# A two-layer encoder trunk on one core: q and k kept by head pair, an epsilon scaled by the frame's mean square, and the softmax sums' tiles moved to another pool

## The chip, the cores and the metric

The kernel runs on one core of one Trainium2 chip. The metric is device time in microseconds (us) of one execution. Engines: TensorE (PE, with its weight loads shown as PEld), VectorE (DVE), ScalarE (ACT), GpSimd (POOL), and SyncE (SP), which issues the DMAs.

## The reference, cut to what matters

Two residual layers on x (512 frames, 1024 channels, float32). Layer 0 mixes tokens with trailing means, layer 1 with chunked attention; each is followed by a gated MLP of 2816 hidden channels with a causal convolution over three frames.

```python
def rmsnorm(x, g):
    y = xf * lax.rsqrt(jnp.mean(xf * xf, axis=-1, keepdims=True) + EPS)      # EPS = 1e-6
    return y * g

def chunk_attention(h, w_qkv, q_norm, k_norm, rel_table, w_o):
    q, k, v = jnp.split(h @ w_qkv, 3, axis=-1)                 # 16 heads of 64
    q = head_rmsnorm(q, q_norm)                                # mean of squares over a head's 64, + EPS
    k = head_rmsnorm(k, k_norm)
    # each chunk of 64 frames attends to its own and the 8 chunks before it
    s = einsum(q, k) * HEAD_DIM ** -0.5 + bias[rel]
    return einsum(softmax(s), v) @ w_o

def conv_ffn(h, w_gate, w_val, conv_w, conv_b, w_out):
    a = causal_dwconv3(h @ w_gate) + conv_b
    return (silu(a) * (h @ w_val)) @ w_out

for i in range(2):
    x = x + mixer_i(rmsnorm(x, mix_norm[i]))
    x = x + conv_ffn(rmsnorm(x, ffn_norm[i]), ...)
```

In layer 1 the attention's input h is x times the frame's factor r = rsqrt(mean square of the frame + EPS) times the gain. Because r is one number for a frame, q and k can be projected from x times the gain alone, and the head norms then take r into account.

## The kernel before, in words

**Arithmetic.** Each matmul in full precision is made of three (`mm3`, L123 to L125): the operands are split into a high and a low part (`split`, L102 and L103: ScalarE copies the high part, VectorE subtracts; `split_scaled`, L107 and L108, does it with a factor), and high times high, high times low and low times high are added up in one bank of PSUM. Moving tiles are 128 x 512 (512 frames, 2048 bytes for each partition).

**FFNs (`ffn`).** The first few of the 22 blocks f of 128 hidden channels are plain products of the normed input (`plain`, 512-wide matmuls only). From f = 5 on Strassen's scheme takes seven products of half size a block (`strassen`, `product`, L594 and L596: four 512-wide matmuls with the high weights and both parts of the moving half, four 256-wide ones with the low weights). Between the products the schedule places matmuls of the output projection of an earlier group of blocks (`output`, names `out`, `ow`, `wo_r`), three or six at a time. All orders of TensorE are written by hand there. The moving tiles are `two` and `h` (normed input), `one` and `u` (hidden values).

**Attention (`attention`).** `opening` projects v by Strassen and the first quarter of q and k (c = 0; a quarter holds four heads of q and the same four of k, 512 columns). `project(c)` does the other quarters while the heads run: `products` issues the matmuls, `evict(t)` copies the bank of frame tile t (128 frames by 512 columns) to `Z[c, t]`, on VectorE for odd t and ScalarE for even t, and puts `squares(t)` and then `norms()` into the list `late`, from which the loop over heads and frame tiles takes one entry after a step. `squares` takes the squares (ScalarE) and sums them by head (VectorE, L1302). `norms` makes the factor: sum times `r2` (r squared over 64, L1317), plus EPS (L1318), rsqrt (L135 to L139), times r (L1320), and GpSimd then multiplies `Z[c, t]` by it for t = 0 to 3 (L1322; L1212 in `opening`). `channel_major(p, i)` transposes pair p (two heads) of q (i = 0) or k (i = 1) on TensorE, four transposes `zt` (L1365) that read the pair's 128 columns from `Z[p // 2, t]`, and splits the result (L107 and L108, or L1369 and L1372).

For each head and frame tile: `scores` (L1395, L1396; bias and maximum on VectorE, L1399; exponential on ScalarE, L1405, which also sums into a column of `sums[p]`), two steps later `turn` (transposes `tp`, L1436, split into `pt`), two more later `mix` (products `oo` with v, L1448). `sums_out`, `sums_in` and `scale` bring the inverse sums to the channels' layout through DRAM. Work that fills TensorE between: quarter 1's rest, quarters 2 and 3, and the output projection `wo`. TensorE's order is written by hand; of the other engines the planner orders the heads' part. Four PSUM banks (tag "S") serve scores, `zt`, `tp`, `rt` and `oo` in turn.

**Memory.** Pools open one behind the other, and a tile's place follows from the sizes of those before it: `consts` (ending at 18,432 bytes for each partition), `wp` (seven tiles of 4096 bytes: raw weights `wr`, and the halves `wh` and `wl`, two each), `act` (`X`, `one`, `two`), then `tmp`: `fill1` (128), five small norm columns and four-column tiles (128 and 128), six `g` tiles of 2048, four `mx` (32 each), two `sums` (32 each). Behind tmp come, at different times, the pools of the start (`pw` and others), of the first FFN (`h`, `gv` and `ow` halves), of the attention (`kl`, `zqk`, then `pre`, then `heads` with `pt`, `B`, `sb`, `o2`, `rs`, `rb`) and of the second FFN. The first FFN's `u` tiles and later `Z` lie in pools counted from the top of memory. `LINE` is 512 and `CONST` 128.

Of the kernel before, what the change touches and what calls it, by code (L numbers as in the profile page):

```python
# [30 lines left out]
HD = 64  # L31
NPAIR = H // 2
TT = S // P
# [3 lines left out]
EPS = 1e-6  # L37
# [4 lines left out]
LINE, CONST = 512, 128  # L42
# [30 lines left out]
def trunk(ctx: ExitStack, tc: tile.TileContext, xt, xT, cols, band, edge, poolw, gv, wout, wqk, wv, wo, rel, out):  # L73
    nc = tc.nc
# [3 lines left out]
    tmp = ctx.enter_context(tc.tile_pool(name="tmp", bufs=1))  # L78
# [62 lines left out]
    def small(name, n, tag="nw"):  # L141
        return tmp.tile([P, n], F32, name=name, tag=f"{tag}{n}", bufs=4)
# [211 lines left out]
    ident = consts.tile([P, P], F32, name="ident")  # L354
# [561 lines left out]
    def attention(rest, hook, hidden_slots):  # L916
        XS = set2
        O2, V, Z, QK, SM = {}, {}, {}, {}, {}
# [9 lines left out]
        def by_frame(v):  # L928
            return v.rearrange("p (t h) -> p t h", t=TT)

        zp = None

        def opening(pre):
# [3 lines left out]
            Y, SQ, sums, form = {}, {}, {}, {}  # L937
# [87 lines left out]
            def lo(n):  # L1025
                part_lo(f"v{n}")
# [33 lines left out]
            zp = closing.enter_context(tc.tile_pool(name="bz", bufs=1, side="right", reuse_waits="tile"))  # L1060
# [5 lines left out]
            ov = [psum("S", f"qk0_{t}", 4) for t in range(TT)]  # L1066
# [64 lines left out]
            a, rcol, t_ = (small(f"n1_{c}", TT) for c in "ayt")  # L1131
# [5 lines left out]
            nc.vector.scalar_tensor_tensor(t_, rcol, -0.5, rcol, op0=OP.mult, op1=OP.mult)  # L1137
            nc.vector.tensor_mul(t_, t_, a)
            nc.vector.scalar_tensor_tensor(rcol, t_, 1.5, rcol, op0=OP.add, op1=OP.mult)
            nc.vector.scalar_tensor_tensor(r2, rcol, 1.0 / HD, rcol, op0=OP.mult, op1=OP.mult)  # L1140
            lo(0)
            query(3)


            ss, a, y, t_ = norms_of(0)
            for t in range(TT):
                Z[0, t] = zp.tile([P, 8, HD], F32, name=f"z0_{t}", tag="z", bufs=8)
            flat = [Z[0, t].rearrange("p h d -> p (h d)") for t in range(TT)]
            zsq = {}

            def square(t):
                zsq[t] = g_tile(f"zs0_{t}")
                nc.scalar.activation(zsq[t], flat[t], AF.Square)

            def reduce(t):
                nc.vector.tensor_reduce(by_frame(ss)[:, t, :], zsq.pop(t).rearrange("p (h d) -> p h d", d=HD), axis=mybir.AxisListType.X, op=OP.add)
# [16 lines left out]
                return [vx(f"{name}{i}") for i in range(2)]  # L1173

            hi(1)
            nc.vector.tensor_copy(flat[1], ov[1])
            nc.scalar.activation(flat[0], ov[0], AF.Copy)
            nc.scalar.activation(flat[2], ov[2], AF.Copy)
            nc.vector.tensor_copy(flat[3], ov[3])
            square(0)  # L1180
            lo(1)
            half(0, A, "a11", True)
# [12 lines left out]
            reduce(2)  # L1195
            reduce(3)
            lo(3)
            nc.vector.tensor_mul(by_frame(a), by_frame(ss), r2[:, :, None].to_broadcast([P, TT, 8]))
            nc.vector.tensor_scalar(a, a, EPS, None, op0=OP.add)
            B = [psum("P", f"vb{i}") for i in range(2)]  # L1200
            half(2, B, "a12", True)
            hi(4)
# [7 lines left out]
            nc.vector.tensor_mul(by_frame(y), by_frame(y), rcol[:, :, None].to_broadcast([P, TT, 8]))  # L1210
            for t in range(TT):
                nc.gpsimd.tensor_mul(Z[0, t], Z[0, t], by_frame(y)[:, t, :, None].to_broadcast([P, 8, HD]))  # L1212
            half(3, B, "a12", True)
            hi(5)
            lo(5)
# [51 lines left out]
            c = pair_of("c12")  # L1267
# [25 lines left out]
        def project(c, banks="PQ", ready=None):  # L1293

            ov = [psum(banks[t // 2], f"qk{c}_{t}", BANKS[banks]) for t in range(TT)]
            ss, a, y, t_ = norms_of(c)
            s3, a3, y3 = (by_frame(v) for v in (ss, a, y))

            def squares(t):
                sq = g_tile(f"zs{c}_{t}")  # L1300
                nc.scalar.activation(sq, Z[c, t].rearrange("p h d -> p (h d)"), AF.Square)
                nc.vector.tensor_reduce(s3[:, t, :], sq.rearrange("p (h d) -> p h d", d=HD), axis=mybir.AxisListType.X, op=OP.add)  # L1302


            def evict(t):
                Z[c, t] = z = zp.tile([P, 8, HD], F32, name=f"z{c}_{t}", tag="z", bufs=8)
                flat = z.rearrange("p h d -> p (h d)")
                if t % 2:
                    nc.vector.tensor_copy(flat, ov[t])
                else:  # L1310
                    nc.scalar.activation(flat, ov[t], AF.Copy)
                late.append(lambda: squares(t))

            yield from products(ov, wqk[c], f"wqk{c}", nc.gpsimd, evict, ready)

            def norms():
                nc.vector.tensor_mul(a3, s3, r2[:, :, None].to_broadcast([P, TT, 8]))  # L1317
                nc.vector.tensor_scalar(a, a, EPS, None, op0=OP.add)  # L1318
                rsqrt(a, y, t_)
                nc.vector.tensor_mul(y3, y3, rcol[:, :, None].to_broadcast([P, TT, 8]))  # L1320
                for t in range(TT):
                    nc.gpsimd.tensor_mul(Z[c, t], Z[c, t], y3[:, t, :, None].to_broadcast([P, 8, HD]))  # L1322

            late.append(norms)

# [33 lines left out]
        def channel_major(p, i):  # L1359


            zt = psum("S", f"zt{p}_{i}", 4)
            for t in range(TT):
                j = 4 * i + 2 * (p % 2)
                nc.tensor.transpose(zt[:, t * P:(t + 1) * P], Z[p // 2, t][:, j:j + 2, :].rearrange("p h d -> p (h d)"), ident)  # L1365
# [12 lines left out]
            for o, x in moves:  # L1378
                nc.sync.dma_start(o.bitcast(F32), x if x.dtype == F32 else x.bitcast(F32))
            QK[p, i] = (zh, z2)  # L1380

        def scores(h, t):

            p, e = divmod(h, 2)
            q, k, kl = QK[p, 0][e], QK[p, 1][e], KL[p % 2][e]
            if t == 0:

                base = rdram[h, :]
                for r, n in ((0, S - HD), (HD, S)):
# [9 lines left out]
            nc.vector.tensor_tensor_reduce(out=s_[:, :n], in0=sc[:, :n], in1=BT[h % 2][:, :n][:, ::-1], scale=1.0,  # L1399
                                           scalar=3e38, op0=OP.add, op1=OP.min, accum_out=mx[:, 0:1])  # L1400
            if p < NPAIR - 1:
                if e == 0 and t == 0:
                    sums[p] = tmp.tile([P, 2 * TT], F32, name=f"sums{p}", tag="sums", bufs=2)
                c = e * TT + t
                nc.scalar.activation(s_[:, :n], s_[:, :n], AF.Exp, scale=-1.0, bias=mx[:, 0:1], accum_out=sums[p][:, c:c + 1])  # L1405
                if c == 2 * TT - 1:
                    nc.vector.reciprocal(sums[p], sums[p])
            else:
                nc.scalar.activation(s_[:, :n], s_[:, :n], AF.Exp, scale=-1.0, bias=mx[:, 0:1], accum_out=mx[:, 1:2])
                nc.vector.reciprocal(mx[:, 2:3], mx[:, 1:2])  # L1410
                nc.scalar.activation(s_[:, :n], s_[:, :n], AF.Copy, scale=mx[:, 2:3])
# [59 lines left out]
        with tc.manual_schedule(engines={mybir.EngineType.PE}):  # L1471
# [17 lines left out]
            for i in range(nb + LAG + LAGM):  # L1489
                steps = []  # L1490
                p = (i - 9) // 8
# [6 lines left out]
                j = i - LAG  # L1498
# [112 lines left out]
```

## Time and profile before

| | |
|---|---|
| time of the runs, us | 972.7, 973.65, 973.53 (median 973.53) |
| time of the profiled execution, us | 972.28 |
| its span, us | 970.5 |
| TensorE busy, share of the span | 99% |
| VectorE busy | 87% |
| ScalarE busy | 59% |
| GpSimd busy | 8% |
| granted TensorE clock | 1.000 |

The span is the time from the first to the last instruction of the profiled execution; 1.8 us of its time lie around it. The parts in order of time: the pool mixer to about 30 us, the first FFN to about 350 with its last outputs to about 372, the attention's opening to about 457, the heads to about 608, the second FFN to the end. In a row of the order of time the first number is the start, the second the time until the end of the row's last instruction; matmuls overlap, so the pace of TensorE is the distance from one start to the next and not the duration.

### The profile page before, as it was taken

The numbers are of one execution on the slowest core, as the hardware profiler recorded it, in microseconds if no ns is written. First come the engines' busy times: TensorE is split into PE (matmuls) and PEld (weight loads), VectorE is DVE, ScalarE is ACT, GpSimd is POOL, SyncE is SP. The second block draws the span as 40 slices with busy tenths as digits, with TensorE's granted clock in tenths as the row PEclk, the third lists the DMA queues.
The fourth block names the chain that finished last, engine by engine and source line by source line (L and its number), as shares of the span: only waits on it lengthen the run. The fifth ranks groups of instructions, "written<-read, shape, count | busy, mean of one in ns | idle before, by whom it ended". The sixth has DMA issues, their size and how long they took to land. (4 is left out here: it accounts for less than half of the span.)

```text
span 970.5 us, 13715 instructions
## 1 busy us (share of the span) xinstructions
PE 960.2 (99%) x4965; PEld 809.0 (83%) x4965; DVE 849.1 (87%) x1479; ACT 575.0 (59%) x980; POOL 80.5 (8%) x76
## 2 busy tenths in 40 slices
PE   8999999999999999999999999999999999999998
PEld 7788988888888888888888787888988888888886
DVE  8999999999899859894776988899999999899853
ACT  7665554655555457465777777656556555465521
POOL 2300000000000000033534310000000000000000
PEclk9999999999999999999999999999999999999999
DMA  9232332332323317024443442232233233233322
GB/s 342 70 99 71 114 108 80 120 119 81 114 79 120 102 47 292 20 66 134 143 122 108 129 118 67 90 121 84 75 114 119 72 121 127 84 103 91 105 82 103
DMA packets 40227, 105.73 MB, mean 109 GB/s; under 512 B 4744, under 2 KB 8272, under 8 KB 40160
## 3 DMA queue, kind: packets, MB, share of 16 engines
q1 hardware_dynamic: 40096, 104.82, 33.3%
q8 instruction: 39, 0.64, 0.3%
q14 instruction: 28, 0.23, 0.1%
q0 software_dynamic: 32, 0.04, 0.0%
q10 hardware_dynamic: 32, 0.00, 0.0%
HBM read 98.48 MB, written 2.17 MB: 104 GB/s over the span
## 5 line engine op out<-in xcount | busy, mean ns | idle before, releaser
L124 PE MATMUL out<-one,ow_h 128*128 128x512 f32 x224 | 88.6, 395 | 0.0
L123 PE MATMUL out<-one,ow_h 128*128 128x512 f32 x224 | 88.5, 395 | 0.0
L125 PE MATMUL out<-one,ow_l 128*128 128x512 f32 x224 | 88.4, 395 | 0.0
L830 DVE TENSOR_TENSOR X<-out,X 128x512 f32<-128x512 f32 (+1 forms) x65 | 44.1, 680 | 47.8 <-PE out L125 47.7
L594 PE MATMUL st_m<-two,g_h 128*128 128x512 f32 x240 | 75.5, 396 | 0.0
L594 PE MATMUL st_m<-h,g_h 128*128 128x512 f32 x240 | 75.1, 394 | 0.0
L393 ACT ACTIVATE ow_h<-wo_r 128x768 fp32r<-128x768 f32 (+1 forms) x56 | 44.5, 795 | 44.7 <-PE out L124 41.9
L408 DVE SCALAR_TENSOR_TENSOR c<-a,col,c 128x511 f32<-128x511 f32 (+1 forms) x76 | 56.4, 744 | 0.0
L594 PEld LDWEIGHTS st_m<-h,g_h 128*128 128x128 f32 x240 | 45.1, 188 | 10.6
L596 PEld LDWEIGHTS st_m<-two,g_l 128*128 128x128 f32 x240 | 45.1, 188 | 10.5
L594 PEld LDWEIGHTS st_m<-two,g_h 128*128 128x128 f32 x240 | 44.0, 188 | 10.5 <-ACT w L603 0.9
L394 DVE TENSOR_TENSOR ow_l<-wo_r,ow_h 128x768 fp32r<-128x768 f32 (+1 forms) x56 | 50.1, 895 | 2.2 <-ACT ow_h L393 2.2
L603 ACT ACTIVATE w<-st_m 128x512 f32<-128x512 f32 x30 | 18.0, 599 | 56.2 <-PE st_m L596 56.2
L596 PE MATMUL st_m<-two,g_l 128*128 128x256 f32 x240 | 47.7, 280 | 0.0
L596 PE MATMUL st_m<-h,g_l 128*128 128x256 f32 x240 | 47.6, 279 | 0.0
L125 PEld LDWEIGHTS out<-one,ow_l 128*128 128x128 f32 x224 | 42.1, 188 | 6.1
L123 PEld LDWEIGHTS out<-one,ow_h 128*128 128x128 f32 x224 | 42.1, 188 | 6.0
L124 PEld LDWEIGHTS out<-one,ow_h 128*128 128x128 f32 x224 | 42.1, 188 | 5.9
L1399 DVE CUSTOM_DVE_ANT_0 sb<-sc,B 128x128 f32<-128x128 f32 (+1 forms) x64 | 31.1, 485 | 15.7 <-PE sc L1396 11.0
L405 ACT ACTIVATE c<-a,col 128x512 f32<-128x512 f32 x38 | 30.7, 812 | 23.1 <-DVE a L752 21.6
L1405 ACT ACTIVATE sb<-sb,mx 128x128 f32<-128x128 f32 (+3 forms) x56 | 31.3, 559 | 17.8 <-DVE mx L1399 16.8
L393 ACT ACTIVATE g_h<-gv_r 128x1024 fp32r<-128x1024 f32 x32 | 33.7, 1054 | 12.3 <-DMA gv_r<-gv 9.8
(464 smaller groups left out, 3004.2 us busy)
## 6 DMA issues: line engine op xcount, KB each, us to landing
gv_r<-gv SPq DMA_DIRECT2D x86, 512.0 KB, 3.6
wo_r<-wout SPq DMA_DIRECT2D x32, 384.0 KB, 3.1
wo_r<-wout SPq DMA_DIRECT2D x32, 320.0 KB, 2.9
wqk_r<-wqk SPq DMA_DIRECT2D x12, 512.0 KB, 3.7
b<-wv SPq DMA_DIRECT2D x8, 512.0 KB, 7.0
wo_r<-wo SPq DMA_DIRECT2D x8, 512.0 KB, 3.4
xt<-xt SPq DMA_DIRECT2D x4, 512.0 KB, 5.9
X<-xT SPq DMA_DIRECT2D x8, 256.0 KB, 7.5
```

Of the source, the lines that this page charges most:

```text
L123: yield nc.tensor.matmul(o, sh, mh, start=first, stop=False, **how)
L124: yield nc.tensor.matmul(o, sh, ml, start=False, stop=False, **how)
L125: yield nc.tensor.matmul(o, sl, mh, start=False, stop=last, **how)
L393: nc.scalar.activation(hi[:, :n], raw[:, :n], AF.Copy)
L394: return hi, lo, lambda: nc.vector.tensor_sub(lo[:, :n], raw[:, :n], hi[:, :n].bitcast(F32))
L405: nc.scalar.activation(c, a, AF.Identity, scale=cw[2], bias=cw[3])
L408: nc.vector.scalar_tensor_tensor(c[:, j:], a[:, :S - j], cw[2 - j], c[:, j:], op0=OP.mult, op1=OP.add)
L594: nc.tensor.matmul(o, hi[:, c], B[i, name], start=first and i == 0, stop=False, **how)
L596: nc.tensor.matmul(o[:, 0], lo[:, c], B[i, name][:, 0], start=False, stop=i == 3, **how)
L830: nc.vector.tensor_add(X[d][:, fs], o[:, fs], X[d][:, fs])
L1399: nc.vector.tensor_tensor_reduce(out=s_[:, :n], in0=sc[:, :n], in1=BT[h % 2][:, :n][:, ::-1], scale=1.0, scalar=3e38, op0=OP.add, op1=OP.m ...
L1405: nc.scalar.activation(s_[:, :n], s_[:, :n], AF.Exp, scale=-1.0, bias=mx[:, 0:1], accum_out=sums[p][:, c:c + 1])
```

## The change

It has three parts. `Z[c]` becomes one tile for a quarter, laid out by group of 128 columns (pair of q, pair of q, pair of k, pair of k), then frame tile, then column; evictions and squares write and read four pieces of 128 columns, a transpose reads one piece, and GpSimd multiplies group by group, for all frames at once, in the order 0, 2, 1, 3. The head norm's factor is made from the sum over 64 plus `eps`, a tile of four columns that holds EPS times the frame's mean square (plus EPS), in one VectorE instruction; the multiplications by `r2` and by r are gone. The `sums` tiles, eight columns each, are taken from the pool `heads`, with 512 bytes each, and no longer from `tmp`.

```diff
+        def variance(a, ss):
+            nc.vector.scalar_tensor_tensor(by_frame(a), by_frame(ss), 1.0 / HD, eps[:, :, None].to_broadcast([P, TT, 8]), op0=OP.mult, op1=OP.add)
+        def normalise(c, y):
+            for g in (0, 2, 1, 3):
+                z = Z[c][:, g].rearrange("p t (e d) -> p t e d", e=2)
+                nc.gpsimd.tensor_mul(z, z, by_frame(y)[:, :, 2 * g:2 * g + 2, None].to_broadcast([P, TT, 2, HD]))
...
-            nc.vector.scalar_tensor_tensor(r2, rcol, 1.0 / HD, rcol, op0=OP.mult, op1=OP.mult)
+            nc.vector.tensor_scalar(eps, a, EPS, None, op0=OP.mult)
...
-                Z[0, t] = zp.tile([P, 8, HD], F32, name=f"z0_{t}", tag="z", bufs=8)
+            Z[0] = zp.tile([P, TT, TT, P], F32, name="z0", tag="z", bufs=2)
+            flat = [Z[0][:, :, t, :] for t in range(TT)]
...
             def evict(t):
-                Z[c, t] = z = zp.tile([P, 8, HD], F32, name=f"z{c}_{t}", tag="z", bufs=8)
+                if t == 0:
+                    Z[c] = zp.tile([P, TT, TT, P], F32, name=f"z{c}", tag="z", bufs=2)
+                z = Z[c][:, :, t, :]
...
             def norms():
-                nc.vector.tensor_mul(a3, s3, r2[:, :, None].to_broadcast([P, TT, 8]))
-                nc.vector.tensor_scalar(a, a, EPS, None, op0=OP.add)
+                variance(a, ss)
                 rsqrt(a, y, t_)
-                nc.vector.tensor_mul(y3, y3, rcol[:, :, None].to_broadcast([P, TT, 8]))
-                for t in range(TT):
-                    nc.gpsimd.tensor_mul(Z[c, t], Z[c, t], y3[:, t, :, None].to_broadcast([P, 8, HD]))
+                normalise(c, y)
...
-                nc.tensor.transpose(zt[:, t * P:(t + 1) * P], Z[p // 2, t][:, j:j + 2, :].rearrange("p h d -> p (h d)"), ident)
+                nc.tensor.transpose(zt[:, t * P:(t + 1) * P], Z[p // 2][:, 2 * i + p % 2, t, :], ident)
...
-                    sums[p] = tmp.tile([P, 2 * TT], F32, name=f"sums{p}", tag="sums", bufs=2)
+                    sums[p] = heads.tile([P, LINE // 4], F32, name=f"sums{p}", tag="sums", bufs=2)[:, :2 * TT]
...
-        r2, late, sums, RB = small("r2", TT), [], {}, {}
+        eps, late, sums, RB = small("eps", TT), [], {}, {}
```

`opening` changes in the same way for c = 0.

More of the change, by code (lines that the diff above doesn't have):

```diff
@@ L929, in by_frame, with heads_of @@
             return v.rearrange("p (t h) -> p t h", t=TT)
+        def heads_of(x):
+            return x.rearrange("p (g d) -> p g d", g=TT)
+        def variance(a, ss):
[4 more added lines that the diff above has]
+                nc.gpsimd.tensor_mul(z, z, by_frame(y)[:, :, 2 * g:2 * g + 2, None].to_broadcast([P, TT, 2, HD]))
         zp = None
@@ L1145, in opening @@
             ss, a, y, t_ = norms_of(0)
-            for t in range(TT):
-                Z[0, t] = zp.tile([P, 8, HD], F32, name=f"z0_{t}", tag="z", bufs=8)
-            flat = [Z[0, t].rearrange("p h d -> p (h d)") for t in range(TT)]
+            Z[0] = zp.tile([P, TT, TT, P], F32, name="z0", tag="z", bufs=2)
+            flat = [Z[0][:, :, t, :] for t in range(TT)]
             zsq = {}
@@ L1152, in square @@
                 zsq[t] = g_tile(f"zs0_{t}")
-                nc.scalar.activation(zsq[t], flat[t], AF.Square)
+                nc.scalar.activation(heads_of(zsq[t]), flat[t], AF.Square)
             def reduce(t):
@@ L1175, in opening @@
             hi(1)
[L1176 to L1179, printed above, removed]
+            nc.vector.tensor_copy(flat[1], heads_of(ov[1]))
+            nc.scalar.activation(flat[0], heads_of(ov[0]), AF.Copy)
+            nc.scalar.activation(flat[2], heads_of(ov[2]), AF.Copy)
+            nc.vector.tensor_copy(flat[3], heads_of(ov[3]))
             square(0)
@@ L1197, in opening @@
             lo(3)
-            nc.vector.tensor_mul(by_frame(a), by_frame(ss), r2[:, :, None].to_broadcast([P, TT, 8]))
-            nc.vector.tensor_scalar(a, a, EPS, None, op0=OP.add)
+            variance(a, ss)
             B = [psum("P", f"vb{i}") for i in range(2)]
@@ L1209, in opening @@
             nc.vector.scalar_tensor_tensor(y, t_, 1.5, y, op0=OP.add, op1=OP.mult)
-            nc.vector.tensor_mul(by_frame(y), by_frame(y), rcol[:, :, None].to_broadcast([P, TT, 8]))
-            for t in range(TT):
-                nc.gpsimd.tensor_mul(Z[0, t], Z[0, t], by_frame(y)[:, t, :, None].to_broadcast([P, 8, HD]))
+            normalise(0, y)
             half(3, B, "a12", True)
@@ L1296, in project @@
             ss, a, y, t_ = norms_of(c)
-            s3, a3, y3 = (by_frame(v) for v in (ss, a, y))
+            s3 = by_frame(ss)
             def squares(t):
                 sq = g_tile(f"zs{c}_{t}")
-                nc.scalar.activation(sq, Z[c, t].rearrange("p h d -> p (h d)"), AF.Square)
+                nc.scalar.activation(heads_of(sq), Z[c][:, :, t, :], AF.Square)
                 nc.vector.tensor_reduce(s3[:, t, :], sq.rearrange("p (h d) -> p h d", d=HD), axis=mybir.AxisListType.X, op=OP.add)
             def evict(t):
-                Z[c, t] = z = zp.tile([P, 8, HD], F32, name=f"z{c}_{t}", tag="z", bufs=8)
-                flat = z.rearrange("p h d -> p (h d)")
+                if t == 0:
+                    Z[c] = zp.tile([P, TT, TT, P], F32, name=f"z{c}", tag="z", bufs=2)
+                z = Z[c][:, :, t, :]
                 if t % 2:
-                    nc.vector.tensor_copy(flat, ov[t])
+                    nc.vector.tensor_copy(z, heads_of(ov[t]))
                 else:
-                    nc.scalar.activation(flat, ov[t], AF.Copy)
+                    nc.scalar.activation(z, heads_of(ov[t]), AF.Copy)
                 late.append(lambda: squares(t))
@@ L1316, in norms @@
             def norms():
-                nc.vector.tensor_mul(a3, s3, r2[:, :, None].to_broadcast([P, TT, 8]))
-                nc.vector.tensor_scalar(a, a, EPS, None, op0=OP.add)
+                variance(a, ss)
                 rsqrt(a, y, t_)
-                nc.vector.tensor_mul(y3, y3, rcol[:, :, None].to_broadcast([P, TT, 8]))
-                for t in range(TT):
-                    nc.gpsimd.tensor_mul(Z[c, t], Z[c, t], y3[:, t, :, None].to_broadcast([P, 8, HD]))
+                normalise(c, y)
             late.append(norms)
@@ L1363, in channel_major @@
             for t in range(TT):
-                j = 4 * i + 2 * (p % 2)
-                nc.tensor.transpose(zt[:, t * P:(t + 1) * P], Z[p // 2, t][:, j:j + 2, :].rearrange("p h d -> p (h d)"), ident)
+                nc.tensor.transpose(zt[:, t * P:(t + 1) * P], Z[p // 2][:, 2 * i + p % 2, t, :], ident)
             zh, z2 = (big.tile([P, S], F32R, name=f"z{c}{p}_{i}", tag="zqk", bufs=8) for c in "h2")
```

## The prediction

> **What bounds the kernel now.** I read the page first: its engine list, then the waits of TensorE, then TensorE's busy time by stretches, and last TensorE's own order of time, start by start.
>
> ```profile
> span 970.5 us, 13715 instructions
> PE 960.2 (99%) x4965; PEld 809.0 (83%) x4965; DVE 849.1 (87%) x1479; ACT 575.0 (59%) x980; POOL 80.5 (8%) x76
> ```
>
> ```profile
> PE zt L1365 <- POOL z L1322: 1.7, 1, 1.7
> ```
>
> ```profile
> 540.00:560.00 20.00, 18.11 (x103) 14.38 (x102) 18.37 (x46) 15.07 (x40) 8.16 (x8) 1.00 0.44 134
> 700.00:800.00 100.00, 100.00 (x535) 85.70 (x535) 95.26 (x152) 57.78 (x85) 0.00 (x0) 1.00 0.31 103
> ```
>
> TensorE is busy for 99% of the span, and the FFN stretches show no gap at all, at a granted clock of 1.00. So only two things move the end: the few waits of TensorE, and the pace at which it starts one matmul after the other where it never waits. The longest wait is for GpSimd's scaling of q and k (L1322); it lies in 540 to 560 us, where TensorE is idle for 20.00 - 18.11 = 1.89 us.
>
> The pace can be read from starts. "Busy" durations (0.39 us) overlap and hide it. In each pair below both rows belong to one unbroken run of 128x512 matmuls:
>
> ```profile
> 609.19 0.39 PE L123 MATMUL wo<-two,wo_h 128*128 128x512 f32 x1
> 619.84 0.39 PE L125 MATMUL wo<-two,wo_l 128*128 128x512 f32 x1
> 620.07 0.40 PE L123 MATMUL gv<-one,gv_h 128*128 128x512 f32 x1
> 629.64 0.39 PE L125 MATMUL gv<-one,gv_l 128*128 128x512 f32 x1
> 937.11 0.39 PE L123 MATMUL out<-one,ow_h 128*128 128x512 f32 x1
> 966.27 0.40 PE L125 MATMUL out<-one,ow_l 128*128 128x512 f32 x1
> 18.99 0.40 PE L124 MATMUL po<-one,pwh 128*128 128x512 f32 x1
> 29.73 0.39 PE L125 MATMUL po<-one,pwl 128*128 128x512 f32 x1
> 335.32 0.40 PE L125 MATMUL out<-one,ow_l 128*128 128x512 f32 x1
> 348.62 0.40 PE L125 MATMUL out<-one,ow_l 128*128 128x512 f32 x1
> ```
>
> The attention's last products (wo) go 47 steps in 10.65 us, 0.2266 us each. The same instruction in the next run (gv, 41 steps in 9.57 us) takes 0.2334; the last out products 0.2333 (125 steps in 29.16), the pool products 0.2335 (46 in 10.74), the first FFN's out products 0.2333 (57 in 13.30). What differs is where the tiles lie. Adding up the pools in the order of the code: consts, wp and act end at multiples of 512 B, and tmp holds 128 (fill1) + 128 + 128 + 6 x 2048 + 128 (mx) + 64 (the two sums tiles) = 25 x 512 + 64 B. So everything in the pools that open behind tmp (h, u of the second FFN, gv and ow halves, pw, kl, zh, pt) starts 64 B past a multiple of 128 B, while X, one, two and wp's tiles start on it. In the first stretch moving tile (two) and weights (wo in wp) have the same offset; in each of the other four the weights sit 64 B off the moving tile (one).
>
> **The change part by part.** *Sums out of tmp, 512 B each in heads.* It moves no instruction. It takes 64 B from tmp, so every pool behind it moves down by 64 B to a multiple of 512. That touches TensorE's pace in three kinds of place.
>
> (a) Runs as above. At 0.2266 the four that take longer lose 41 x 0.0068 + 125 x 0.0067 + 46 x 0.0069 + 57 x 0.0067 = 0.28 + 0.84 + 0.32 + 0.38 = 1.8 us. The plain gate and value products alternate two (on the line) and h (off it):
>
> ```profile
> 56.64 0.40 PE L123 MATMUL gv<-two,gv_h 128*128 128x512 f32 x1
> 86.93 0.39 PE L125 MATMUL gv<-h,gv_l 128*128 128x512 f32 x1
> 643.56 0.40 PE L123 MATMUL gv<-two,gv_h 128*128 128x512 f32 x1
> 676.62 0.40 PE L125 MATMUL gv<-h,gv_l 128*128 128x512 f32 x1
> ```
>
> 131 steps in 30.29 us and 143 in 33.06: 0.2312 each, so 0.0046 x 274 = 1.26 us more. Against it: a run needs some steps to settle. Behind the transposes of f_rb (46.60), in a run whose tiles all lie on the line, nine steps still took 0.232:
>
> ```profile
> 46.60 0.60 PE L159 MATMUL f_rb<-ident,f_y 128*128 128x128 f32 x4
> 47.27 0.40 PE L124 MATMUL gv<-one,two 128*128 128x512 f32 x1
> 49.36 0.39 PE L124 MATMUL gv<-one,two 128*128 128x512 f32 x1
> ```
>
> Six runs x 10 steps x 0.005 = 0.3 us. I take (a) as 2.75 us; its ends are 0 (the cause is not the offset) and 3.1.
>
> (b) Strassen groups: four 512-wide and four 256-wide matmuls, and in most of them three 512-wide out matmuls between. Never yet have all tiles of such a group lain on one offset, so this has no row of its own. The nearest rows are the twelve 256-wide ones of g4, which lies in tmp's g tiles at 384 B past 512 (a multiple of 128):
>
> ```profile
> 706.53 0.28 PE L123 MATMUL st_t<-two,g_h 128*128 128x256 f32 x1
> 707.01 0.28 PE L124 MATMUL st_t<-two,g_h 128*128 128x256 f32 x1
> 707.25 0.28 PE L123 MATMUL st_t<-h,g_h 128*128 128x256 f32 x1
> 707.81 0.28 PE L125 MATMUL st_t<-h,g_l 128*128 128x256 f32 x1
> ```
>
> With two (equal offset by 128 B) four steps take 0.48, 0.120 each; with h (64 B off) five take 0.56, 0.112 each. So equal offsets are cheaper for 512-wide matmuls and dearer for 256-wide ones. A group at equal offsets would be 7 x 0.2266 + 4 x 0.120 = 2.066 us. Now:
>
> ```profile
> 866.28 0.62 PE L594 MATMUL st_b<-two,g_h 128*128 128x512 f32 x2
> 883.00 0.63 PE L594 MATMUL st_t<-two,g_h 128*128 128x512 f32 x2
> 700.00:925.00 225.00, 66.10 (x419) 64.17 (x420) 1.00 0.31 102
> ```
>
> Eight groups in 16.72 us are 2.090 each. The last row counts L596's weight loads, 420 or 105 groups in one FFN. The second FFN gives 105 x 0.024 = 2.5 us. In the first one u lies in a pool counted from the top of memory, 32 B off a multiple of 128, and stays; its tiles are the moving ones of the out products during six of the fifteen wide f's, so 63 groups count: 1.5 us. I take (b) as 4.0 us, by the rows of 512 and 256 width above. Its ends: 7 x 0.2333 + 4 x 0.120 = 2.113, a loss of 168 x 0.023 = 3.9 us; and 7 x 0.2266 + 4 x 0.112 = 2.034, a gain of 168 x 0.056 = 9.4 us.
>
> (c) Attention: runs of three between transposes, too short to settle by the row of 46.60; 0, between -0.5 and +0.5 us.
>
> The Trainium skill (SBUF — State Buffer, Who interferes with whom) says that TensorE reads moving operand and weights through two independent ports, and that only the port pair shared by VectorE and GpSimd causes contention. By that rule where two tiles lie would cost nothing, and (a) and (b) would be 0. The runs at 0.2266 and 0.2333, the same instruction on the same engine, speak against it; no row says by which mechanism.
>
> *Z by head pair, scaled in order of use.* GpSimd still issues four multiplies per set; now the first covers the q pair that is transposed first, for all frames, where today the transposes of one pair need all four.
>
> ```profile
> 547.42 0.18 DVE L1318 TENSOR_SCALAR qk_a<-qk_a 128x32 f32<-128x32 f32 x1
> 550.37 0.19 DVE L1320 TENSOR_TENSOR qk_y<-qk_y,n_y 128x32 f32<-128x32 f32 x1
> 550.63 5.03 POOL L1322 TENSOR_TENSOR z<-z,qk_y 128x512 f32<-128x512 f32 x4 [4.53 <-DVE qk_y L1320]
> 553.08 1.68 DVE L103 TENSOR_TENSOR wo_l<-wo_r,wo_h 128x1024 fp32r<-128x1024 f32 x1
> 553.28 0.79 PE L1365 MATMUL zt<-ident,z 128*128 128x128 f32 x3
> 554.69 0.55 DVE L1399 CUSTOM_DVE_ANT_0 sb<-sc,B 128x384 f32<-128x384 f32 x1
> 555.72 0.33 PE L1365 MATMUL zt<-ident,z 128*128 128x128 f32 x1 [1.65 <-POOL z L1322]
> 556.09 0.69 ACT L107 ACTIVATE zh<-zt,gq 128x512 fp32r<-128x512 f32 x1
> 556.81 0.75 DVE L108 SCALAR_TENSOR_TENSOR zl<-zt,gq,zh 128x512 f32<-128x512 f32 x1 [0.96 <-ACT zh L107]
> 558.05 0.38 PE L1436 MATMUL tp<-ident,sb 128*128 128x128 f32 x2
> ```
>
> One multiply of four is about 5.03 / 4 = 1.3 us, so the first ends near 551.9, before the transposes at 553.28, and the second (the k pair) near 553.2, before its own four (557 today). The wait goes: up to 1.9 us. What is late next: the scores of t = 3 reuse the bank that L1399 reads (554.69 to 555.24, behind the 1.68 us of wo_l), then the transposes tp x2 reuse the bank of zt and need L108, which waits for L107, which ScalarE's queue puts behind the exponentials of that L1399. L107 would start some 0.4 us earlier (555.7), L108 end near 557.1, and tp start near 557.2 in place of 558.05. I take 0.9 us; ends 0.3 and 1.95. The copies and squares write and read the same 512 columns as four pieces; they lie beside a busy TensorE: 0, and even 0.6 us more on each would not be waited for before 553. GpSimd's copies z2 queue behind all four multiplies as today. A multiply with three free dimensions could be slower; at 2.6 us each, twice today's mean, the k pair is still ready at 555.8.
>
> *Eps by the mean square.* Two small VectorE instructions fewer per set (L1318 and L1320, 0.18 + 0.19), one changed form; r2 becomes eps one for one. Four sets: 1.5 us of VectorE, off the path except before 550.63, where it starts GpSimd 0.37 us earlier; counted above.
>
> **Sum.** 2.75 + 4.0 + 0.9 = 7.65 us. The profiled execution took 972.28 us (span 970.5 and 1.8 around it), which gives 964.6; it stands 1.25 us under the median of 973.53, which gives 965.9.
>
> **The rivals.** *Only long runs settle.* Groups change width every four matmuls, as the row at 46.60 needs about ten to settle. For it: no mixed stretch in this trace runs at the low pace. Against: 0.2266 and 0.120 are both whole steps of one period of 13.3 ns (17 and 9), so widths need not disturb each other. 973.53 - 2.75 - 0.9 = 969.9.
>
> *Groups settle at the better 256-wide pace too:* 9.4 in place of 4.0 for (b): 960.5. Against it: the four steps at 0.120.
>
> *The shift does nothing,* as the skill's rule would have it; the stretches at 0.2333 have another reason (the pool of their weights, say). 973.53 - 0.9 = 972.6, within 0.2% of before, which is about what a measurement of this kernel can tell from no change.
>
> *Slower.* Groups keep 0.2333 for 512-wide matmuls and pay 0.120 for 256-wide ones: +3.9 us at 168 groups; and the runs of (a) do not settle either: 973.53 + 3.9 - 0.9 = 976.5. It decides from a group pace of 2.095 us upward. The 256-wide row speaks for it, the 512-wide ones against.
>
> *VectorE becomes the bound* in the FFNs: it is busy for 95.26 of 100 us now, and 1.2% less time makes that 96.4; still under 1. If its order leaves waits, half of (b) goes: 968.
>
> **How the numbers follow.** The forecast 0.50, with a range of its own from 964 to 968; long runs only 0.20; VectorE 0.05; the better pace 0.08; nothing from the shift 0.12; slower 0.05. From 962 to 971.5 leaves out the better pace, the slower case and most of "nothing". Faster by over 0.2% (under 971.6): 0.50 + 0.20 + 0.05 + 0.08 and a little of the rest, 0.84; within 0.2%: 0.11; slower: 0.05.
>
> **What would show it.** Starts in TensorE's order of time: the last out products 125 steps in 28.3 us in place of 29.16; eight groups in 16.5 us in place of 16.72; 256-wide steps at 0.120. The wait of zt for z gone from the waits of TensorE, and a short one of tp, scores or zt for VectorE near 555 in its place. L1322's four multiplies about as long as now. Wrong: a group pace of 2.09 or more, or long runs still at 0.2333 with all tiles on the line.

## The result and the profile after

The changed kernel takes 967.07 us (median; 967.01 to 968.37) against 973.12 us for the kernel before on the same chip (972.13 to 973.65): ratio 0.9944, 95% interval 0.9929 to 0.996. The forecast was 965.9. Executions in which the chip granted a lower clock throughout are left out of all times below. The profiled execution took 967.01 us, its span 965.2; against the profiled one of before, 972.28 and 970.5, that is 5.3 us less.

The page of the changed kernel, first its span and two rows by stretches, then the wait of TensorE that is new:

```profile
span 965.2 us, 13717 instructions
PE 955.8 (99%) x4965; PEld 810.5 (84%) x4965; DVE 847.8 (88%) x1471; ACT 576.2 (60%) x980; POOL 79.4 (8%) x76
```

```profile
540.00:560.00 20.00, 19.08 (x111) 15.28 (x110) 19.37 (x47) 15.01 (x40) 7.48 (x8) 1.00 0.45 135
700.00:800.00 100.00, 100.00 (x535) 86.03 (x534) 96.61 (x155) 58.08 (x85) 0.00 (x0) 1.00 0.33 107
```

```profile
PE sc L1400 <- DVE mx L1404: 0.8, 1, 0.8
```

TensorE issues the same 4965 matmuls. The wait of `zt` for `z` is gone; in 540 to 560 us TensorE is idle for 0.92 us in place of 1.89. The FFN stretch still has no gap, and VectorE is at 96.61 of 100 us there (95.26 before).

TensorE's order of time, first and last start of the unbroken runs (the same instructions as in the prediction's fence):

```profile
606.59 0.39 PE L123 MATMUL wo<-two,wo_h 128*128 128x512 f32 x1
617.24 0.39 PE L125 MATMUL wo<-two,wo_l 128*128 128x512 f32 x1
617.47 0.39 PE L123 MATMUL gv<-one,gv_h 128*128 128x512 f32 x1
626.76 0.40 PE L125 MATMUL gv<-one,gv_l 128*128 128x512 f32 x1
932.65 0.39 PE L123 MATMUL out<-one,ow_h 128*128 128x512 f32 x1
960.99 0.39 PE L125 MATMUL out<-one,ow_l 128*128 128x512 f32 x1
640.64 0.39 PE L123 MATMUL gv<-two,gv_h 128*128 128x512 f32 x1
673.05 0.39 PE L125 MATMUL gv<-h,gv_l 128*128 128x512 f32 x1
```

`wo` still takes 10.65 us for 47 steps. `gv` now takes 9.29 for 41 (9.57 before), the last out products 28.34 for 125 (29.16), the plain products of the second FFN 32.41 for 143 (33.06): 0.2266 to 0.2267 us a step.

Matching the two traces matmul by matmul, from start to start, gives where the 5.3 us came from:

| stretch (time in the trace of before) | change, us | forecast |
|---|---|---|
| long runs and plain products (19-30, 57-87, 335-349, 620-630, 643-677, 937-967) | -3.00 | -2.75 |
| Strassen groups of the wide f's (108-335, 700-937) | -1.60 | -4.0 |
| stretches with 256-wide matmuls only and a few out (87-108, 677-700) | +0.58 | not in the sum |
| the stall: 552-556 | -2.15 | -0.9, both rows |
| behind it: 556-565 | +1.06 | |
| all else, the start included | -0.17 | 0 |

Strassen groups, one after the other:

```profile
862.44 0.62 PE L594 MATMUL st_b<-two,g_h 128*128 128x512 f32 x2
865.46 0.39 PE L596 MATMUL st_t<-two,g_l 128*128 128x256 f32 x2
865.69 0.39 PE L596 MATMUL st_t<-h,g_l 128*128 128x256 f32 x2
865.92 0.40 PE L123 MATMUL out<-u2h,ow_h 128*128 128x512 f32 x1
866.16 0.39 PE L124 MATMUL out<-u2l,ow_h 128*128 128x512 f32 x1
866.39 0.39 PE L125 MATMUL out<-u2h,ow_l 128*128 128x512 f32 x1
866.61 0.62 PE L594 MATMUL st_m<-two,g_h 128*128 128x512 f32 x2
867.07 0.61 PE L594 MATMUL st_m<-h,g_h 128*128 128x512 f32 x2
867.52 0.40 PE L596 MATMUL st_m<-two,g_l 128*128 128x256 f32 x2
879.13 0.63 PE L594 MATMUL st_t<-two,g_h 128*128 128x512 f32 x2
```

Eight groups, 862.44 to 879.13, take 16.69 us; 16.72 before, forecast 16.5. Inside, the three out matmuls behind the 256-wide ones take 0.69 us (0.230 each), the next four 0.91 (0.2275). Only the end of a run of seven reaches the pace of the long runs.

The stall, rows of the timeline from three engines:

```profile
548.29 4.07 POOL L941 TENSOR_TENSOR z<-z,qk_y 128x512 f32<-128x512 f32 x4 [3.72 <-DVE sums L1412]
551.46 1.99 DVE L103 TENSOR_TENSOR wo_l<-wo_r,wo_h 128x1024 fp32r<-128x1024 f32 x1
551.79 0.60 PE L1370 MATMUL zt<-ident,z 128*128 128x128 f32 x4
553.37 0.54 DVE L1404 CUSTOM_DVE_ANT_0 sb<-sc,B 128x384 f32<-128x384 f32 x1
553.98 0.50 PE L1400 MATMUL sc<-zh,zh 128*128 128x512 f32 x1 [0.77 <-DVE mx L1404]
```

All four transposes go at 551.79, while GpSimd is still multiplying (until 552.36). Then the scores wait 0.77 us for the bank that VectorE reads at L1404, which stands behind 1.99 us of `wo_l`.

### The profile page after: what moved, and what is told of

Its sections match the earlier page's. It is cut to its first block, busy times and chain, and to the rows that moved or that the text cites. A ratio compares the mean times of both kernels' runs of the same rounds, so it can differ in the third digit from the quotient of the medians.

```text
span 965.2 us, 13717 instructions
## 1 busy us (share of the span) xinstructions
PE 955.8 (99%) x4965; PEld 810.5 (84%) x4965; DVE 847.8 (88%) x1471; ACT 576.2 (60%) x980; POOL 79.4 (8%) x76
## 3 DMA queue, kind: packets, MB, share of 16 engines
HBM read 98.48 MB, written 2.17 MB: 104 GB/s over the span
## 4 chain that ended last, share of the span: by engine, by line
PE 95%; DVE 3%; ACT 1%; issue 0%; DMA 0%; DVEq 0%
PE st_m L594 11%; PE out L124 8%; PE out L123 8%; PE out L125 8%; PE st_m L596 6%; PE st_t L594 6%; PE gv L124 4%; PE gv L125 4%; PE gv L123 4%; PE qk L125 3%; PE qk L123 3%; PE qk L124 3%; PE st_t L596 3%; PE st_b L594 3%; PE oo L1453 2%; PE tp L1441 2%
## 5 line engine op out<-in xcount | busy, mean ns | idle before, releaser
L1404 DVE CUSTOM_DVE_ANT_0 sb<-sc,B 128x128 f32<-128x128 f32 (+1 forms) x64 | 31.0, 485 | 16.8 <-PE sc L1401 15.9
L393 ACT ACTIVATE g_h<-sa 128x1024 fp32r<-128x1024 f32 x32 | 33.9, 1058 | 11.9 <-DVE sa L639 7.3
```

The costliest lines, as they stand in the source:

```text
L393: nc.scalar.activation(hi[:, :n], raw[:, :n], AF.Copy)
```

## The experiments

**The two halves of the change alone.** e1 is the kernel before with one line of the change:

```diff
-                    sums[p] = tmp.tile([P, 2 * TT], F32, name=f"sums{p}", tag="sums", bufs=2)
+                    sums[p] = heads.tile([P, LINE // 4], F32, name=f"sums{p}", tag="sums", bufs=2)[:, :2 * TT]
```

> The kernel before with one line changed: the sums tiles come from heads, 512 B each. Z, the norms and GpSimd's order are as before. Theory (where the tiles lie sets TensorE's pace): all of the long runs' and the Strassen groups' gain is here, measured between the two traces as 5.28 - 1.1 = 4.2 us, so about 968.9 us; the last out products (125 steps) take 28.3 us and not 29.16; TensorE's wait for z near 553 stays at 1.7 us. Rival (the tiles' place does nothing, the gain comes from the norms): 973, long runs at 0.2333 a step.

e2 is the changed kernel with that line as before (the `+` and `-` above exchanged).

> The changed kernel with the sums tiles back in tmp (two of 32 B), so that every pool behind tmp starts 64 B past a multiple of 512 again; Z by head pair, scaling in order of use and eps stay. Theory: only the wait for z is gained, 1.1 us net of what comes late next: about 972.0 us, long runs back at 0.2333 a step. Rival (tiles' place does nothing): 967 to 968.

e1 took 969.9 us (968.25 to 970.76), ratio to before 0.9966, interval 0.9953 to 0.998. e2 970.79 us (970.6 to 971.86), ratio 0.9978, interval 0.9969 to 0.9987; before, on this chip, 973.02. In the traces e1 has every gain in the runs and groups of the table to within 0.04 us and none at 552 to 556; e2 has the two rows of the stall, -2.17 and +1.09, and none of the other gains above 0.2. So the moved tiles work by their place alone, and the two parts do not touch each other.

Both medians stand aside from the traces: e2's trace is 1.4 us shorter than that of before, its median 2.2. e1's own trace shows why, in its rows by stretches behind the wait for `z` (PEclk is the third number from the end):

```profile
554.00:555.00 1.00, 0.66 (x2) 0.61 (x3) 0.47 (x1) 0.75 (x3) 0.29 (x1) 0.69 0.33 95
555.00:556.00 1.00, 1.00 (x4) 0.75 (x3) 0.42 (x1) 0.62 (x2) 0.33 (x1) 0.50 1.02 321
556.00:557.00 1.00, 1.00 (x4) 0.71 (x4) 0.33 (x1) 0.20 (x1) 0.28 (x1) 0.50 0.37 127
557.00:558.00 1.00, 1.00 (x7) 0.80 (x5) 0.80 (x3) 0.00 (x0) 0.00 (x0) 0.60 0.52 119
```

```profile
554.35 0.47 PE L1365 MATMUL zt<-ident,z 128*128 128x128 f32 x1 [1.65 <-POOL z L1322]
555.54 0.78 PE L125 MATMUL wo<-two,wo_l 128*128 128x512 f32 x1
```

Right behind the wait of 1.65 us the granted clock falls to 0.50; the shares of the clock that are missing, 0.31 + 0.50 + 0.50 + 0.40, make 3.4 us at half clock. It costs some 1.6 us in 552 to 565 against the trace of before, where the same wait had no such dip. Over all executions with the wait whose mean clock is known, 15 of 42 of the kernel before show 0.997 or 0.998 (973.36 to 975.99 us), 27 show 0.999 or 1.000 (971.82 to 973.48), and e1 has three of the first kind (969.9 to 970.76) and two of the second (968.25, 968.88). Of the 11 executions of e2 and the four of the changed kernel, none is under 0.999. How often it happens differs from chip to chip (6 of 15 executions of before on the chip of e1 and e2, none of 7 on another), so the fair comparison is on one chip: 6 of 15 with the wait against none of e2's 11.

**What counts in the offset.** Three shifts of the changed kernel: e3 moves all pools behind `act` by 128 B, e7 by 256 B, and e4 moves everything that is counted from the bottom of memory, `X`, `one`, `two` and the weights' ring included, by 64 B. Each was executed once.

```diff
-    tmp.tile([P, 32], F32, name="fill1")
+    tmp.tile([P, 64], F32, name="fill1")        # e3; e7 has 96
...
-    consts.tile([P, (LINE - CONST) // 4], F32, name="fill0")
+    consts.tile([P, (LINE - CONST) // 4 + 16], F32, name="fill0")        # e4
```

> The changed kernel with fill1 128 B longer, so that g tiles and every pool behind tmp lie 128 B further: h, u, ow, gv and pw start at 128 past a multiple of 512, one, two, X and wp's tiles at 0. Theory (what counts is the difference of the two operands' offsets modulo 128 B): no change, 967 us, last out products 0.2266 a step. Rival (multiples of 512 B count): as with the sums in tmp, 971 us, 0.2333 a step.

> The changed kernel with fill0 64 B longer, so that every tile counted from the bottom of memory, X, one, two and wp's included, starts 64 B past a multiple of 128; only u of the first FFN and Z, counted from the top, stay. Theory (the difference of moving tile and weights counts, not the place itself): 967 us, long runs at 0.2266. Rival (each operand must itself start on a line): all runs at 0.2333 or worse, the wo products and v products too, 973 us or more.

> The changed kernel with 256 B more in tmp ahead of its other tiles, so that every pool behind it lies 256 B past a multiple of 512 while X, one, two and the weights' ring stay. If equal offsets modulo 256 are what counts, the gains stay: last out products at 0.2266 us a step, 967.1 us. If they must be equal modulo 512, the long runs go back to 0.2333, the last out products take 29.16 us again, and the run takes 969.5 us, as with the shift of 128 B.

e3: 969.53 us; e4: 966.9; e7: 966.88. The last out products, first e3's first and last start, then e7's:

```profile
934.35 0.40 PE L123 MATMUL out<-one,ow_h 128*128 128x512 f32 x1
963.51 0.40 PE L125 MATMUL out<-one,ow_l 128*128 128x512 f32 x1
```

```profile
932.54 0.39 PE L123 MATMUL out<-one,ow_h 128*128 128x512 f32 x1
960.87 0.39 PE L125 MATMUL out<-one,ow_l 128*128 128x512 f32 x1
```

29.16 us at 128 B, as before the change; 28.33 at 256 B. e4 has 28.33 too. So it is the difference of the two operands' places that counts: the low pace came at differences of 0 and 256 B, and not at 64 or 128. Equal modulo 128, which the prediction took, is not enough; equal modulo 256 fits all that was measured. e3's groups gained about as much in sum as the changed kernel's (108 to 318: -0.86 against -0.42; 700 to 925: -0.42 against -0.95), but by another road: in the second FFN e3's 512-wide steps average 0.2322 us (changed kernel 0.2308, before 0.2327) and its 256-wide ones 0.1172 (0.1181 and 0.1172). The place counts in the groups too, and what it gains for one width it loses for the other.

**Why the groups gained so little.** e5 makes all matmuls of a wide group 512 columns wide; it computes the products of the two low parts besides (one execution).

```diff
-                    nc.tensor.matmul(o[:, 0], lo[:, c], B[i, name][:, 0], start=False, stop=i == 3, **how)
+                    nc.tensor.matmul(o, lo[:, c], B[i, name], start=False, stop=i == 3, **how)
```

> The changed kernel, but every matmul of the wide Strassen groups is 512 columns wide: the low weights are multiplied with both parts (the product of the two low parts is computed besides), so a group has eight 512-wide product matmuls, and no width changes inside it or towards the out matmuls. Theory (a change of width unsettles the pace): with all widths equal each step settles at 0.2266 us as in the long runs, a group of 11 takes 2.493 us against 2.090, and the run comes to 967.1 + 210 x 0.403 = 1051.8 us. Rival (the groups miss the low pace for another reason, the alternation of tiles or the work of the other engines): the steps stay at 0.2325 on average, a group takes 2.558 us and the run 1065 us.

e5 took 1054.97 us. In its timeline:

```profile
961.44 0.62 PE L594 MATMUL st_m<-two,g_h 128*128 128x512 f32 x2
962.34 0.62 PE L596 MATMUL st_m<-two,g_l 128*128 128x512 f32 x2
963.25 0.39 PE L124 MATMUL out<-one,ow_h 128*128 128x512 f32 x1
963.93 0.61 PE L594 MATMUL st_t<-two,g_h 128*128 128x512 f32 x2
```

A group, 961.44 to 963.93, takes 2.49 us for eleven steps, 0.2264 each. Over the wide f's of the second FFN the product matmuls average 0.2277 and the out matmuls 0.2274 us; in the changed kernel the 512-wide ones average 0.2308, before 0.2327. (In the first FFN, where the moving tiles `u` of some out products lie 32 B off, the averages are 0.2281 and 0.2297; that is most of the 3 us above the expected time.) Tiles, banks and VectorE's work are the same, so the alternation of tiles does not keep the groups from the low pace; what went is the change of width. VectorE has a fifth more time for a group here, so e5 alone does not clear VectorE's work; e12 below, at the usual length, does.

e10 goes for the 256-wide steps: the low weights in the shared ring lie 64 B off, for 480 of 1176 such matmuls.

```diff
+        def pair(p, tag, bufs, name):
+            hi = p.tile([P, 1024], F32R, name=f"{name}_h", tag=f"{tag}h", bufs=bufs)
+            lo = p.tile([P, 1024 + 64], F32R, name=f"{name}_l", tag=f"{tag}l", bufs=bufs)
+            at = 16 if name[0] == "g" and name[2] == "_" and int(name[3:]) in WIDE else 0
+            return hi, lo[:, at:at + 1024]
...
-                hi, lo = (wp.tile([P, 1024], F32R, name=f"{name}_{c}", tag=f"w{c}", bufs=2) for c in "hl")
+                hi, lo = pair(wp, "w", 2, name)
```

The other tiles of that tag get the same length, and `fill0` and the sums' tiles are cut by 256 B each to make room.

> The changed kernel with the low weights of the wide Strassen groups 64 B past a multiple of 256 where they lie in the ring that all stages share, which is the case for 480 of the 1176 256-wide matmuls; everything else that TensorE reads keeps its offset modulo 256. By the step of the prediction (each matmul has the pace of its own offsets; 0.112 us for 256 columns at 64 B off) these 480 save 0.006 us each against the 0.118 of the changed kernel, 2.9 us: 964.2 us. If the change of width inside the group keeps every step from settling (the other theory), they save no more than the 0.001 us by which the kernel before, with mixed offsets, was faster in these steps: 966.6 us.

e10 took 967.16 us (966.9 to 967.74), as the changed kernel. In the second FFN the shifted steps average 0.1180 us and the others 0.1179. A pace of 0.112 for 256 columns at 64 B off does not show in these groups.

e11 and e12 keep all instructions and have fewer changes of width:

```diff
-                for i, c in enumerate(cs):
-                    nc.tensor.matmul(o, hi[:, c], B[i, name], start=first and i == 0, stop=False, **how)
-                for i, c in enumerate(cs):
-                    nc.tensor.matmul(o[:, 0], lo[:, c], B[i, name][:, 0], start=False, stop=i == 3, **how)
+                swap = name in ('b22', 't4')             # e12: 't1' too
+                low = [(o[:, 0], lo[:, c], B[i, name][:, 0]) for i, c in enumerate(cs)]
+                high = [(o, hi[:, c], B[i, name]) for i, c in enumerate(cs)]
+                both_ = low + high if swap else high + low
+                for i, (x_, w_, m_) in enumerate(both_):
+                    nc.tensor.matmul(x_, w_, m_, start=first and i == 0, stop=i == 7, **how)
+                paired[0] = name in ('b11', 'b21')       # e12: 't3' too
...
-                    if at > wait:
+                    if at > wait and not paired[0]:
```

> The changed kernel with the same instructions of TensorE in another order: in the wide Strassen groups b22 and t4 start with their four 256-wide matmuls, and no out matmul stands between b11 and b22 or b21 and t4, so two blocks of four 256-wide matmuls lie together and the out matmuls come seven or eight at a time behind them. Per f of seven products there are 10 changes of width in place of 14. Theory (each change of width unsettles the pace): against the steps of the run with all matmuls 512 wide, a group of the changed kernel loses 4 x 0.0021 + 3 x 0.0060 = 0.026 us at two changes, 0.013 each; 4 x 30 x 0.013 = 1.6 us less, 965.5 us, with the out matmuls near 0.229 in place of 0.2329. Rival (what counts is not the number of changes): 967.1 us. If VectorE or ScalarE come too late for the closer products, TensorE shows waits in the FFNs and the time grows.

> As the run with two pairs, and t3 with t1 besides: 8 changes of width per f in place of 14. Theory: 6 x 30 x 0.013 = 2.4 us less than the changed kernel, 964.7 us. Rival: 967.1 us. The copy of t2's result has only t3 and four out matmuls to hide behind, 1.9 us in place of 2.8: if it comes late, waits of t1's matmuls for ScalarE appear and eat the gain.

e11 took 969.58 us (969.29 to 970.06), e12 968.53 (968.34 to 968.82): both slower than the changed kernel, by 2.5 and 1.5 us (by the spans of the traces 2.6 and 1.8). e12's waits and timeline:

```profile
PE st_t L598 <- DVE g_l L708: 2.4, 4, 0.6
```

```profile
872.28 0.40 PE L598 MATMUL st_m<-two,g_l 128*128 128x256 f32 x2
872.76 0.63 PE L598 MATMUL st_m<-two,g_h 128*128 128x512 f32 x2
873.69 0.39 PE L123 MATMUL out<-one,ow_h 128*128 128x512 f32 x1
875.05 0.62 PE L598 MATMUL st_m<-two,g_h 128*128 128x512 f32 x2
875.96 0.40 PE L598 MATMUL st_m<-two,g_l 128*128 128x256 f32 x2
876.91 0.63 PE L598 MATMUL st_m<-two,g_h 128*128 128x512 f32 x2
```

Behind the block of eight 256-wide matmuls the next four 512-wide ones take 0.93 us (872.76 to 873.69, 0.2325 each), the six after them 1.36 (0.2267), the last four 0.91 (0.2275). Sorted by their place behind a change of width, e12's 512-wide steps average 0.2334, 0.2349, 0.2295, 0.2322, 0.2313 us and from the sixth on 0.2273 to 0.2280. That is the settling: five steps. In the second FFN of the changed kernel, where blocks of 512-wide steps are seven long, places one to seven average 0.2336, 0.2352, 0.2304, 0.2331, 0.2304, 0.2271 and 0.2274. The 256-wide ones do the reverse: the first behind a change takes 0.1140, the later ones a median of 0.119 to 0.120, which is their settled pace. The theory's part came true: the 512-wide steps of the wide f's take 1.7 us less than in the changed kernel in e11 (expected 1.6) and 2.6 in e12 (expected 2.4). The price was elsewhere. In both, t4 begins with g4's low weights, which are split last, and TensorE waits for them in four places; those four steps are together 3.1 us longer than settled ones. And the other 256-wide steps, settled for longer, take 0.9 us more. A version in which t4 keeps its order in those places was not run.

**What took the stall away.** Three runs of the changed kernel: e6 and e8 with GpSimd's multiplies in another order, e9 with eps added as before but the order of use kept. e8 and e9 were executed once each.

```diff
-            for g in (0, 2, 1, 3):
+            for g in (1, 3, 0, 2):        # e6; e8 has (1, 3, 2, 0)
...
-            nc.vector.scalar_tensor_tensor(by_frame(a), by_frame(ss), 1.0 / HD, eps[:, :, None].to_broadcast([P, TT, 8]), op0=OP.mult, op1=OP.add)
+            nc.vector.tensor_mul(by_frame(a), by_frame(ss), eps[:, :, None].to_broadcast([P, TT, 8]))        # e9, and below
+            nc.vector.tensor_scalar(a, a, EPS, None, op0=OP.add)
...
-        def normalise(c, y):
+        def normalise(c, y, r):
+            nc.vector.tensor_mul(by_frame(y), by_frame(y), r[:, :, None].to_broadcast([P, TT, 8]))
...
-            nc.vector.tensor_scalar(eps, a, EPS, None, op0=OP.mult)
+            nc.vector.scalar_tensor_tensor(eps, rcol, 1.0 / HD, rcol, op0=OP.mult, op1=OP.mult)
```

> The changed kernel with GpSimd's four multiplies in the order 1, 3, 0, 2, so that the pairs that are transposed first are scaled last. Theory (the wait went by the order of use): TensorE waits for z again, 1.3 to 1.7 us at the first transposes, and the run is about 1.1 us longer than the changed kernel, 968.2 us. Rival (the wait went by the two VectorE instructions fewer and the earlier start of GpSimd, 0.4 us): the wait stays gone or is at most 0.5 us, and the time stays at 967.1 us.

> The changed kernel with GpSimd's multiplies in the order 1, 3, 2, 0: the q pair that is transposed first is scaled last of all, so its transposes need all four multiplies, as they did before the change. Theory A (the earlier start of GpSimd and the 1.0 us that its four multiplies save by lying elsewhere are enough, the order is not needed): the last multiply ends some 0.6 us after the transposes could start, TensorE waits about 0.6 us for z, its next wait, of the scores for mx, shrinks from 0.8 to about 0.2, and the 13 us from 552 to 565 take the same 12.1 us as in the changed kernel; 967 us. Theory B (the order of use is what pays): the wait for z is back at over 1 us and the run is 1 us longer than the changed kernel.

> The changed kernel with eps added as before, so two small VectorE instructions more per set ahead of GpSimd's multiplies, but with q and k by head pair and in order of use. Theory A (with the order of use GpSimd has time enough): GpSimd starts 0.4 to 0.9 us later by TensorE's clock, the first pair is still ready before its transposes, no wait for z comes back, 967 us. Theory B (the earlier start is what took the wait away): TensorE waits for z again by 0.5 to 1.5 us, and the 13 us from 552 to 565 take about 1 us more than in the changed kernel.

e6 took 968.06 us (967.03 to 968.35), ratio to before 0.9955, interval 0.9938 to 0.9972, and no wait for `z`: 552 to 565 gains 1.06 us as in the changed kernel (1.09). Its profiled execution is 1.1 us longer than the changed kernel's, of which 0.87 lies in the first 19 us. The expectation that the wait returns was wrong: in this order the q pair is the third, ready in time, and the k pair's transposes come later.

e8 took 967.4 us. In this order the first transposes need all four multiplies; its TensorE rows:

```profile
552.32 0.66 PE L1370 MATMUL zt<-ident,z 128*128 128x128 f32 x4 [0.51 <-POOL z L941]
553.88 0.50 PE L1400 MATMUL sc<-zh,zh 128*128 128x512 f32 x1
```

The wait for `z` is 0.51 and the scores' wait is gone; 552 to 565 gains 0.64 us. e9 took 967.51 us. Its GpSimd row:

```profile
549.77 5.05 POOL L942 TENSOR_TENSOR z<-z,qk_y 128x512 f32<-128x512 f32 x4 [4.63 <-DVE qk_y L939]
```

GpSimd starts at 549.77, about where the kernel before has it (550.63) once e9's lead of 0.9 us in TensorE's order is taken off, and takes 5.05 us again, yet no wait for `z` comes back, and 552 to 565 gains 1.18 us. (Another wait, 0.5 us for VectorE in the value projection at 428 us, stands in this execution alone.) So with `Z` by head pair the order of use does the whole by itself, and the shorter norm without that order does 0.64 of 1.1: it starts GpSimd 0.8 us earlier by TensorE's order, where its four multiplies take 4.07 us. The kernel before has one long multiply, the fourth:

```profile
553.64 2.02 POOL L1322 TENSOR_TENSOR z<-z,qk_y 128x512 f32<-128x512 f32 x1
```

The other three take 1.04 to 1.05 us each. The fourth comes while VectorE works on `wo_l` (553.08 to 554.76), and it is the one that the last transpose waits for; e9's fourth, beside `wo_l` again, takes 2.03. In the changed kernel all four start before `wo_l` does, and each takes 1.05.

## Why the prediction was right, and where it was not

*Place of the tiles (a): right in cause and size.* 3.00 us for 2.75, by e1 alone; of the 0.3 us allowed for settling under 0.1 was needed. "Equal by 128 B" was wrong and did no harm, since the change makes them equal modulo 512. The rule that only the port pair of VectorE and GpSimd causes contention (the Trainium skill, SBUF — State Buffer, Who interferes with whom) does not describe what the kernel before, e3 and e7 measure: 29.16, 29.16 and 28.33 us for the same 125 steps at differences of 64, 128 and 256 B.

*Strassen groups (b): the mis-sized term.* Forecast 4.0 us, measured 1.60, and 0.58 lost in the stretches beside them. The step that failed is "a group at equal offsets would be 7 x 0.2266 + 4 x 0.120". Both paces are those of settled runs, and e12 shows them inside groups (0.2273 to 0.2280, 0.119 to 0.120). But a run of seven 512-wide matmuls spends five on settling, so the changed kernel's 512-wide steps average 0.2308 us (0.2327 before). The prediction had charged ten steps of settling to each long run and none to the groups; "only long runs settle", its rival at 969.9, was nearer on this term than the forecast, and the truth lies between: seven steps are enough for the last two. The 256-wide steps got dearer as foreseen (from 0.1172 to 0.1181 us on average), and where they stand nearly alone (87 to 108, 677 to 700), which the sum left out, that is the 0.58. Of the signs named for this term, eight groups in 16.5 us did not come (16.69), and the pace of a group, 2.086 us, stays only just under the 2.09 that was to show the forecast wrong.

*The stall: right, 0.9 forecast and 1.09 measured, with the named successors:* the scores' wait for the bank of L1404 behind `wo_l` (0.77 us). The multiply of 1.3 us was a mean of three of 1.05 and one of 2.02; the first two were ready in time either way. What was not foreseen: the eps part, counted only as 0.37 us of earlier start, would without the order of use have brought more than half of the gain (e8), and with the wait went the dips of the clock that about a third of the executions of before show (e1's trace has one right behind the wait; e2, without it, has none). That is the likely reason why the medians differ by 6.05 us and the two profiled executions by 5.3; no trace of before with a dip is kept.

*VectorE as the bound* did not come: 96.61 of 100 us, and no gap. *Slower* would have needed 2.095 us a group; it is 2.086 in the stretch shown.

By the traces, 7.65 us were forecast and 5.3 came: 2.4 less on the groups and 0.6 lost beside them, against 0.25 more on the runs, 0.2 on the stall and 0.2 elsewhere. The time is nearer, 967.07 for 965.9, because the forecast was set against a median of 973.53, which lies among the executions with a dip (973.36 and up) and not among those without (up to 973.48), while the profiled execution took 972.28. That part of the agreement is luck: by the profiled execution the forecast was 964.6.

## What to carry to other kernels

Where TensorE never waits, read its starts, not its busy share: two runs of the same instruction at 0.2266 and 0.2333 us differ only in where moving tile and weights lie, and padding that makes the two equal modulo 256 B costs no instruction. It makes 256-wide steps dearer (0.117 to 0.120), so count both widths. A pace read in a long run holds in a mixed sequence only after some five equal steps, so give each stretch of one width its own settling before multiplying; and a reordering that lengthens such stretches must be charged with whatever then comes late. A wait of TensorE can cost more than its length when the clock falls behind it: compare the granted clock of several executions with and without the wait before trusting one trace.

## What the runs showed of the hardware that was not expected

- The pace of 512-wide matmuls depends on the difference of their operands' places: 0.2267 us at 0 and 256 B (changed kernel, e7), 0.2333 at 64 and 128 (before, e3), and 0.2267 again when both move by 64 B together (e4). 256-wide ones go the other way: 34 of them in a row from 673.51 us on take 0.120 each in the changed kernel, and about 0.117 in the kernel before.
- Behind a change of width 512-wide matmuls need five steps to reach that pace; the first 256-wide one is short, 0.114 us, the later ones 0.119 to 0.120 (e12). No run tells by which mechanism.
- A wait of 1.65 us was followed by 3.4 us at clock 0.50 in e1's trace. The Trainium skill (TensorE: Matmul & The Clock Gate, Part 1: The HAM clock gate) says that a monitor looks at free-running windows of 3413 ns and halves the clock after an idle one. The length agrees, and windows that run free would explain that the same wait is followed by it in some executions only; but here a wait of half a window was enough. The clock's changes in e1's trace (4.84, 554.38, 557.80 us) do lie on a grid of 3.413 us. On that grid e1's wait fills the end of a window in which TensorE is idle for 1.72 us in all; the wait of before, which no dip follows, lies in the beginning of one with 1.65. Idle time alone does not separate the cases: the window of e2 that holds the end of its last matmul has 1.88 us idle, and the clock falls only one window later. What decides is not shown.
- VectorE's `wo_l` took 1.99 us beside GpSimd's multiplies, which kept 1.05 us each, in the changed kernel, and 1.68 in the kernel before, where a multiply took 2.02. The same instruction without them takes 1.22, as in the timeline of before:

```profile
542.40 1.22 DVE L103 TENSOR_TENSOR wo_l<-wo_r,wo_h 128x1024 fp32r<-128x1024 f32 x1
```

The Trainium skill (SBUF — State Buffer, Who interferes with whom) has the two engines share one port pair, for which a VectorE instruction with two inputs in SBUF contends with GpSimd's reads; this agrees with it.
